# A streaming-encoder block on one core: a wider ramp in four stages, other rates for the adaLN tiles, and gate rows by way of DRAM

## The chip, the cores and the metric

The kernel runs on one core of one Trainium2 chip. The metric is the device time of one execution in microseconds, and the median of several executions stands for a kernel. The engines are TensorE (PE, with its weight loads shown as PEld), VectorE (DVE), ScalarE (ACT), GpSimd (POOL) and SyncE (SP). Lines such as L174 are lines of the kernel's source.

## The reference

One layer with three sublayers, over 256 tokens of 2048 channels in float32. Each sublayer normalises x, modulates it with a shift and a scale that come from the condition c by a large matrix (adaLN), and adds its result, multiplied by a gate that comes from c too.

```python
mod = (jax.nn.silu(c) @ w_ada[l] + b_ada[l]).reshape(B, N_SUBLAYERS, 3, D_MODEL)
shift, scale, gate = mod[:, :, 0], mod[:, :, 1], mod[:, :, 2]

def modulate(h, s):
    return _layer_norm(h) * (1.0 + scale[:, s, None, :]) + shift[:, s, None, :]

y = _swiglu(modulate(x, 0), ffn1_w13[l], ffn1_w2[l])
x = _layer_norm(ALPHA * x + FFN_WEIGHT * gate[:, 0, None, :] * y, ln_g[l, 0], ln_b[l, 0])

u = modulate(x, 1)
proj = u @ w_in[l] + b_in[l]
...
y = jnp.concatenate([h_m, h_r], axis=-1) @ w_out[l]
x = _layer_norm(ALPHA * x + gate[:, 1, None, :] * y, ln_g[l, 1], ln_b[l, 1])

y = _swiglu(modulate(x, 2), ffn2_w13[l], ffn2_w2[l])
x = _layer_norm(ALPHA * x + FFN_WEIGHT * gate[:, 2, None, :] * y, ln_g[l, 2], ln_b[l, 2])
```

`_swiglu` is `(silu(u @ w1) * (u @ w3)) @ w2` with 5632 inner columns. The mixer between the two FFNs makes q, k, v and gates of an mLSTM (four heads) and of a gated linear recurrence (RG-LRU) from one projection.

## The kernel before

**Weight tiles.** Every weight is read once, in tiles of 128 x 2048 float32 (1 MB). `load` (L81) takes one of four buffers named raw and issues the DMA on SP's queue; `split` (L88) makes a high part on ACT (L95) and the rest, a low part, on DVE (L97). High and low parts have three buffers each. A product is three matmuls: high by high, low by high, high by low (`mov_t`, L279, and L625 to L627 in the ramp). So a tile of the FFNs gives 24 matmuls of 128x128 by 128x512. Products collect in the eight PSUM banks.

**adaLN tiles.** The condition's matrix comes as 144 tiles of 1 MB, each with the 128 columns of one (sublayer, shift/scale/gate, channel tile) for all 2048 inputs. `ada_tile` (L170) loads one into a raw buffer, by the same queue, and DVE multiplies it by the broadcast silu(c) (`scb`, made at L148 to L155) and sums along the row (L174): one column of `adac`. Their order is fixed: for each sublayer the 32 of shift and scale, then the 16 of the gate. They are strewn among the weight tiles: `load` calls `tick` (L182), which adds the present rate to a credit and loads one adaLN tile for each whole credit. `ada_until` (L177) loads, at once, all that are still missing up to a given one. The rates are RAMP_RATE, FFN1_RATE, MIX_RATE and FFN2_RATE; FFN1's credit is set to zero after its last but one group, and the mixer and FFN2 begin at -2.

**Ramp.** FFN1 can't begin with a whole contraction, since that needs shift and scale of all 16 channel tiles. So the first 24 of its 44 tiles of inner columns (12 units of 512 columns, gate parts and value parts by turns, in 6 blocks) are done in five stages over 2, 3, 3, 4 and 4 channel tiles. After each stage a unit's partial sum is added to a home in SBUF: the two halves of `yacc`, `gate`, and x itself, which is reloaded later (`fetch`, L678). Units 0 and 1 stay in PSUM. `modulate` (L233) makes the modulated, transposed and split inputs for the next stage, two units before a stage ends, after an `ada_until` for that stage. In the last stage blocks 0 to 3 go through `gated` (silu on ACT, product on DVE) and, two tiles later, `turn` (transposes on PE, split on ACT and DVE). Blocks 4 and 5 do so in `g1(2)`.

**FFN after the ramp.** Groups of eight inner tiles: `g1` makes a group's inner activations, `g2` of the group before multiplies them by w2 and adds to `yacc`. At the last but one group `gate_rows` spreads the gate to all partitions, and `residual` (L322) adds gate times `yacc` to x. The last tiles are handled by `boundary` (L343), an order written out by hand: last products, residual, LayerNorm, modulation for the next sublayer and its first products.

**Gate rows.** `gate_rows` (L189) calls `rows_of` four times: each makes 512 columns of the broadcast gate row by four fp32 matmuls of a stretched column by the identity, and ACT copies the bank to `gate`. It is called three times; `rows_of` also makes `scb`.

**Mixer.** Output gates (w_vo), 25 projection tiles of one kind (`proj`, L796, with 16 x 2 matmuls each), gates and recurrence on DVE and ACT among them; then `ada_until` for the gate's columns and `gate_rows` (L931), v, k, q with the heads, and 16 tiles of w_out. Before the last four w_out tiles stands an `ada_until` for all of the third sublayer's shift and scale (L1041).

Each engine's instructions run in one order, which a planner with a model of times sets before the run; only the instructions of the boundaries and some others are pinned to the program's order.

Of the kernel before, what the change touches and what calls it, by code (L numbers as in the profile page):

```python
# [11 lines left out]
F32 = mybir.dt.float32  # L12
# [39 lines left out]
def block_kernel(ctx: ExitStack, tc: tile.TileContext, a: dict, out: bass.AP):  # L52
# [5 lines left out]
    sm = ctx.enter_context(tc.tile_pool(name="sm", bufs=4))  # L58
    ph = ctx.enter_context(tc.tile_pool(name="ph", bufs=1))

    def slot(name, dtype=F32):
# [79 lines left out]
    def rows_of(ps, col):  # L141

        for k in range(4):
            nc.tensor.matmul(ps[:, k * P:(k + 1) * P], col[:, k:k + 1].to_broadcast([P, P]), ident,
                             start=True, stop=True)

# [42 lines left out]
    def gate_rows(s, weight):  # L189

        for n in range(4):
            ps = bank(f"adag{s}{n}")
            rows_of(ps, adac[:, s, 2, 4 * n:4 * n + 4])
            nc.scalar.mul(gate[:, n * 512:(n + 1) * 512], ps, weight)

# [336 lines left out]
    def ffn(s, w13, w2, start, following=None):  # L532
# [23 lines left out]

        def gated(b, g, v):

            hth, htl = hts[4 * b // GRP]
            i = 4 * b % GRP  # L560
            sgs = []
            for t in range(NT):
                sg = sm.tile([P, 512], F32, tag="u", bufs=2, name=f"sg{s}{b}{t}")
                nc.scalar.activation(sg, g[t], AF.Silu)
                nc.vector.tensor_mul(sg, sg, v[t])
                sgs.append(sg)

            def turn():
                for t in range(NT):
                    tk = slice(t * P, (t + 1) * P)  # L570
                    ps = bank(f"th{b}{t}")
                    for j in range(4):
                        nc.tensor.transpose(ps[:, j * P:(j + 1) * P], sgs[t][:, j * P:(j + 1) * P], ident)
                    ps = ps.rearrange("p (a b) -> p a b", a=4)
                    nc.scalar.copy(hth[:, i:i + 4, tk], ps)
                    nc.vector.tensor_sub(htl[:, i:i + 4, tk], ps, hth[:, i:i + 4, tk].bitcast(F32))

            later(2, turn)

        units = RAMP // 2  # L580
        room = [r[:, 512 * i:512 * (i + 1)] for r in (*yacc, gate) for i in range(4)]
        room += [x[:, i // 4, 512 * (i % 4):512 * (i % 4 + 1)] for i in range(8)]
        part = [None, None] + [room[2 * i:2 * i + 2] for i in range(units - 2)]

        def ramp(ns):

            kept = {}
            n_w = k0 = 0
            ns, rest = ns()
            for st, k in enumerate(STAGES):  # L590
# [54 lines left out]
                for q in range(units):  # L645
# [11 lines left out]
                    if q not in kept:  # L657
                        for ps, p in zip(pss, part[q]):
                            if first:
                                nc.scalar.copy(p, ps)  # L660
                            else:
                                nc.vector.tensor_add(p, p, ps)
                    if last and q % 2 and q < 8:
                        gated(q // 2, *(kept.get(i) or part[i] for i in (q - 1, q)))
                k0 += k

        def g1(gi):
            grp = groups[gi]
            if start and gi == 2:
                new_h(gi)  # L670
                gated(4, part[8], part[9])
                later(4, lambda: (gated(5, part[10], part[11]), fetch()))
                return
            for b in range(grp[0] // 4, grp[-1] // 4 + 1):
                if b or start:
                    rows_block(b)

        def fetch():  # L678

            if True:  # L680
                with tc.issue_after(evac[-1].ins):
                    nc.scalar.dma_start(bq, a["b_s"])
                    nc.scalar.dma_start(rgp, a["rgp"])
                for t in range(NT):
                    nc.scalar.dma_start(x[:, t, :], a["x"][t * P:(t + 1) * P, :])
                scale_x()

# [40 lines left out]
        for gi in range(done, len(groups)):  # L728
# [438 lines left out]
```

## Time and profile before

| | |
|---|---|
| runs | 1980.02, 1989.11, 1979.78 us, median 1980.02 |
| profiled execution | 1983.66 us, of which span 1981.9 us |
| mean granted TensorE clock | 0.982 |
| DMA | 512.71 MB, mean 259 GB/s |
| adaLN reductions on DVE (L174) | 144, 338.9 us |

The span is cut into 40 slices of 49.5 us in the page's second part, where each digit is a busy share in tenths. In the lists of groups a row gives line, engine, operation, output and inputs with their shapes, how often, busy time and mean ns of one, and the idle time of the engine before them with what ended it. In the list of waits a row gives who waited for whom, the sum in us, how often, and the longest. Rows of the queues give the start and length of an issue; several in a row are merged, with their count.

### The profile page before, as it was taken

What the parts mean: (1) busy time and instruction counts of PE and PEld (TensorE: products, weight loads), DVE (VectorE), ACT (ScalarE), POOL (GpSimd) and SP (SyncE); (2) the same over time, 40 slices, a digit from 0 to 9 for tenths busy, and PEclk for the clock granted to TensorE, in tenths of its full rate; (3) what the DMA queues carried; (4) which work ended last, traced back from release to release, by engine and by line L of the source; (5) the groups of instructions that cost most, each with busy time, mean ns of one, the idle gap of its engine ahead of it and who ended that gap; (6) DMA issues with size and microseconds to landing.
All of it is one profiled execution on the core that took longest, in us unless ns stands there. A gap on an engine that the chain in (4) does not pass through costs nothing.

```text
span 1981.9 us, 21425 instructions
## 1 busy us (share of the span) xinstructions
PE 1895.1 (96%) x8680; PEld 1566.3 (79%) x8680; DVE 1422.6 (72%) x1360; ACT 846.1 (43%) x813; POOL 36.5 (2%) x59
## 2 busy tenths in 40 slices
PE   6999999999999999999899958999999999999997
PEld 5788888888878887788688846788888888888885
DVE  7899997867767668699987796556655644544656
ACT  5434444534333345655543317543444333334340
POOL 0000000000000000000000120000000000000000
PEclk8999999999999999999999989999999999999998
DMA  9999888878777564588886685566666655554552
GB/s 376 343 349 338 317 306 327 316 284 309 297 298 283 219 228 172 217 302 314 317 317 255 232 322 208 195 250 252 226 258 248 235 198 187 189 195 178 191 213 85
DMA packets 72675, 512.71 MB, mean 259 GB/s; under 512 B 8448, under 2 KB 8576, under 8 KB 10880
## 3 DMA queue, kind: packets, MB, share of 16 engines
q1 hardware_dynamic: 70848, 507.54, 68.5%
q10 hardware_dynamic: 1728, 3.80, 0.6%
q8 instruction: 68, 1.11, 0.2%
q14 instruction: 31, 0.25, 0.0%
HBM read 509.22 MB, written 2.10 MB: 258 GB/s over the span
## 4 chain that ended last, share of the span: by engine, by line
PE 67%; DVE 13%; DMA 11%; issue 6%; ACT 3%; POOL 0%; DVEq 0%; SPq 0%; ACTq 0%
DMA ada<-in_w_ada 10%; PE fv L287 5%; PE fv L288 5%; PE fv L286 5%; PE py L287 4%; PE py L286 4%; PE py L288 4%; PE fg L288 4%; PE fg L287 4%; PE fg L286 4%; PE rp L626 4%; PE rp L625 4%; PE rp L627 4%; DVE ada L174 3%; PE pj L276 3%
## 5 line engine op out<-in xcount | busy, mean ns | idle before, releaser
L174 DVE CUSTOM_DVE_ANT_0 ada<-ada,scb,badac 128x2048 f32<-128x2048 f32 x144 | 338.9, 2358 | 101.1 <-DMA ada<-in_w_ada 99.4
L97 DVE TENSOR_TENSOR lw<-rw,hw 128x2048 fp32r<-128x2048 f32 x80 | 183.1, 2291 | 123.3 <-ACT hw L95 123.3
L95 ACT CAST hw<-rw 128x2048 fp32r<-128x2048 f32 x80 | 153.1, 1913 | 239.7 <-PE py L288 116.1
L97 DVE TENSOR_TENSOR lfv<-rfv,hfv 128x2048 fp32r<-128x2048 f32 x64 | 146.2, 2291 | 132.8 <-ACT hfv L95 132.8
L95 ACT CAST hfg<-rfg 128x2048 fp32r<-128x2048 f32 (+1 forms) x64 | 117.0, 1833 | 203.4 <-PE fv L288 83.8
L287 PE MATMUL fv<-lfv,u 128*128 128x512 f32 x512 | 200.4, 391 | 3.3 <-DVE lfv L97 3.3
L95 ACT CAST hfv<-rfv 128x2048 fp32r<-128x2048 f32 x64 | 122.4, 1913 | 189.0 <-PE fg L288 145.0
L286 PE MATMUL fv<-hfv,u 128*128 128x512 f32 x512 | 199.3, 390 | 2.3 <-ACT hfv L95 2.3
L97 DVE TENSOR_TENSOR lfg<-rfg,hfg 128x2048 fp32r<-128x2048 f32 x60 | 137.2, 2290 | 88.3 <-ACT hfg L95 88.3
L288 PE MATMUL fv<-hfv,u 128*128 128x512 f32 x512 | 199.8, 390 | 0.0
L286 PE MATMUL py<-hw,hth 128*128 128x512 f32 x512 | 199.7, 391 | 0.0
L287 PE MATMUL py<-lw,hth 128*128 128x512 f32 x512 | 199.4, 389 | 0.1
L288 PE MATMUL py<-hw,htl 128*128 128x512 f32 x512 | 199.3, 389 | 0.0
L287 PE MATMUL fg<-lfg,u 128*128 128x512 f32 x496 | 193.7, 391 | 1.1 <-DVE lfg L97 1.1
L286 PE MATMUL fg<-hfg,u 128*128 128x512 f32 x496 | 194.6, 392 | 0.0
L288 PE MATMUL fg<-hfg,u 128*128 128x512 f32 x496 | 193.6, 390 | 0.0
L276 PE MATMUL pj<-u,hs 128*128 128x512 f32 x512 | 180.5, 398 | 0.0
L95 ACT CAST hra<-rra 128x2048 fp32r<-128x2048 f32 (+1 forms) x51 | 92.1, 1812 | 131.0 <-PE rp L627 71.3
L277 PE MATMUL pj<-u,ls 128*128 128x256 f32 x512 | 142.9, 280 | 0.0
L625 PE MATMUL rp<-hra,u 128*128 128x512 f32 x320 | 124.1, 396 | 6.9 <-ACT hra L95 5.2
L626 PE MATMUL rp<-lra,u 128*128 128x512 f32 x320 | 125.6, 394 | 0.7 <-DVE lra L97 0.7
L627 PE MATMUL rp<-hra,u 128*128 128x512 f32 x320 | 125.2, 393 | 0.0
(362 smaller groups left out, 3431.8 us busy)
## 6 DMA issues: line engine op xcount, KB each, us to landing
ada<-in_w_ada SPq DMA_DIRECT2D x144, 1024.0 KB, 5.4
rw<-in_w SPq DMA_DIRECT2D x80, 1024.0 KB, 4.8
rfg<-in_w SPq DMA_DIRECT2D x64, 1024.0 KB, 4.8
rfv<-in_w SPq DMA_DIRECT2D x64, 1024.0 KB, 4.8
rra<-in_w_r SPq DMA_DIRECT2D x48, 1024.0 KB, 6.4
rs<-in_w_s SPq DMA_DIRECT2D x32, 1024.0 KB, 4.9
rwo<-in_w_out SPq DMA_DIRECT2D x16, 1024.0 KB, 5.1
ro<-in_w_vo SPq DMA_DIRECT2D x8, 1024.0 KB, 4.8
```

Source lines behind the costliest of these rows:

```text
L95: act.copy(cut(hi, w), like(raw[:, w], hi))
L97: low.tensor_sub(cut(lo, w), like(raw[:, w], lo), cut(hi, w).bitcast(F32))
L174: nc.vector.tensor_tensor_reduce(raw, raw, scb, 1.0, badac[:, s, j, kt:kt + 1], ALU.mult, ALU.add, adac[:, s, j, kt:kt + 1])
L276: nc.tensor.matmul(ps, hi[:, w], u2[:, k].rearrange("p w b -> p (w b)"), start=k == 0, stop=False)
L277: nc.tensor.matmul(ps[:, 0:S], lo[:, w], uh[:, k, :], start=False, stop=k == KT - 1)
L286: nc.tensor.matmul(o, acth[:, k0 + j, tk], cut(hi, w), start=first and j == 0, stop=False)
L287: nc.tensor.matmul(o, acth[:, k0 + j, tk], cut(lo, w), start=False, stop=False)
L288: mm = nc.tensor.matmul(o, actl[:, k0 + j, tk], cut(hi, w), start=False, stop=last and j == 3)
L625: nc.tensor.matmul(pss[t], uh[:, k0 + j, tk], hi[:, w], start=a0 and j == j0, stop=False)
L626: nc.tensor.matmul(pss[t], uh[:, k0 + j, tk], lo[:, w], start=False, stop=False)
L627: mm = nc.tensor.matmul(pss[t], ul[:, k0 + j, tk], hi[:, w], start=False, stop=a1 and j == j0 + nj - 1)
```

## The change

Seven things change together.

- The ramp takes 32 inner tiles (16 units, 8 blocks) in four stages over 2, 4, 5 and 5 channel tiles. Blocks 6 and 7, which `g1(3)` used to make, move into it.
- The homes of the partial sums are two spare slots (blocks 1 and 2), `yacc[0]`, `gate`, `yacc[1]` and both halves of x (blocks 3 to 7). In the last stage blocks 4 to 7 are gated in place, and their `turn` comes in `g1(2)` and `g1(3)`. The second half of the inner activations' slots is taken in block 2's `turn`. x is reloaded at `g1(3)`.
- The rates of adaLN tiles per weight tile are others: the ramp's, 0.68 for 0.6 in FFN1 and 0.76 for 0.55 in the mixer.
- The credit is no longer set to zero after the FFNs' last but one group.
- `gate_rows` makes one transpose of the 16 gate columns, one small ACT multiplication, a DMA of the 16 x 128 result to a line in DRAM and a DMA that reads that line into all 128 partitions; both are issued by POOL.
- `rows_of`, now only for `scb`, uses transposes in place of matmuls.
- At the start the first adaLN tile and b_ada are issued ahead of x.

```diff
-STAGES = (2, 3, 3, 4, 4)
-RAMP = 24
+STAGES = (2, 4, 5, 5)
+RAMP = 32
...
-RAMP_RATE = (1.0, 0.67, 0.89, 0.67, 0.6)
-FFN1_RATE = 0.6
-MIX_RATE = 0.55
+RAMP_RATE = (1.0, 0.63, 0.6, 0.6)
+FFN1_RATE = 0.68
+MIX_RATE = 0.76
...
         for k in range(4):
-            nc.tensor.matmul(ps[:, k * P:(k + 1) * P], col[:, k:k + 1].to_broadcast([P, P]), ident,
-                             start=True, stop=True)
+            nc.tensor.transpose(ps[:, k * P:(k + 1) * P], col[:, k:k + 1].to_broadcast([P, P]), ident)
...
     def gate_rows(s, weight):
-        for n in range(4):
-            ps = bank(f"adag{s}{n}")
-            rows_of(ps, adac[:, s, 2, 4 * n:4 * n + 4])
-            nc.scalar.mul(gate[:, n * 512:(n + 1) * 512], ps, weight)
+        pt = bank(f"adag{s}")
+        nc.tensor.transpose(pt[0:KT, 0:P], adac[:, s, 2, :], ident)
+        row = sm.tile([KT, P], F32, tag="grow", bufs=1, name=f"grow{s}")
+        nc.scalar.mul(row, pt[0:KT, 0:P], weight)
+        line = dram.tile([1, D], F32, name=f"line{s}")
+        nc.gpsimd.dma_start(line.rearrange("o (k p) -> (o k) p", p=P), row)
+        nc.gpsimd.dma_start(gate, line.to_broadcast([P, D]))
...
         units = RAMP // 2
-        room = [r[:, 512 * i:512 * (i + 1)] for r in (*yacc, gate) for i in range(4)]
-        room += [x[:, i // 4, 512 * (i % 4):512 * (i % 4 + 1)] for i in range(8)]
-        part = [None, None] + [room[2 * i:2 * i + 2] for i in range(units - 2)]
+        blocks = RAMP // 4
+        room, sgs = {}, {}
+
+        def rooms():
+
+            extra = [slot(f"extra{i}")[:, 0:D] for i in range(2)]
+            homes = [None, extra[0], extra[1], yacc[0], gate, yacc[1], x[:, 0, :], x[:, 1, :]]
+            for b in range(1, blocks):
+                q4 = [homes[b][:, 512 * i:512 * (i + 1)] for i in range(4)]
+                room[2 * b], room[2 * b + 1] = q4[0:2], q4[2:4]
...
                 if last:
                     new_h(0)
-                    new_h(1)
...
-                    if last and q % 2 and q < 8:
-                        gated(q // 2, *(kept.get(i) or part[i] for i in (q - 1, q)))
+                    if last and q % 2:
+                        b = q // 2
+                        g, v = (kept.get(i) or room[i] for i in (q - 1, q))
+                        if b == 2:
+                            gated(b, g, v, fresh=1)
+                        elif b < 4:
+                            gated(b, g, v)
+                        else:
+                            sgs[b] = room[9] if b == 5 else g
+                            for t in range(NT):
+                                nc.scalar.activation(sgs[b][t], g[t], AF.Silu)
+                                nc.vector.tensor_mul(sgs[b][t], sgs[b][t], v[t])
...
-            if start and gi == 2:
+            if start and gi in (2, 3):
                 new_h(gi)
-                gated(4, part[8], part[9])
-                later(4, lambda: (gated(5, part[10], part[11]), fetch()))
+                b = 2 * gi
+                later(1, lambda: turn(b, sgs[b]))
+                later(3, lambda: turn(b + 1, sgs[b + 1]))
+                if gi == 3:
+                    later(3, fetch)
                 return
...
                 if gi == len(groups) - 2:
-                    credit[:] = 0.0, 0.0
                     for t in range(NT):
...
     def start():
+        nc.scalar.dma_start(badac.rearrange("p a b c -> p (a b c)"), a["b_ada"])
+        nc.vector.tensor_scalar_add(badac[:, :, 1, :], badac[:, :, 1, :], 1.0)
+        ada_tile()
         for t in range(NT):
             for c in range(0, D, 1024):
                 nc.sync.dma_start(x[:, t, c:c + 1024], a["x"][t * P:(t + 1) * P, c:c + 1024])
-        nc.scalar.dma_start(badac.rearrange("p a b c -> p (a b c)"), a["b_ada"])
-        nc.vector.tensor_scalar_add(badac[:, :, 1, :], badac[:, :, 1, :], 1.0)
```

`turn` was a function inside `gated` and is now one beside it, so that the ramp's later blocks can call it by themselves; what it does is the same.

More of the change, by code (lines that the diff above doesn't have):

```diff
@@ L555, in rows_block, with gated, turn @@
             gated(b, pg, pv)
-        def gated(b, g, v):
+        def gated(b, g, v, fresh=None):
+            sg = []
+            for t in range(NT):
+                w = sm.tile([P, 512], F32, tag="u", bufs=2, name=f"sg{s}{b}{t}")
+                nc.scalar.activation(w, g[t], AF.Silu)
+                nc.vector.tensor_mul(w, w, v[t])
+                sg.append(w)
+            later(2, lambda: turn(b, sg, fresh))
+        def turn(b, sg, fresh=None):
+            if fresh is not None:
+                new_h(fresh)
@@ L559, in gated @@
             hth, htl = hts[4 * b // GRP]
             i = 4 * b % GRP
-            sgs = []
             for t in range(NT):
[L563 to L576, printed above, removed]
@@ L578, in gated @@
-            later(2, turn)
-        units = RAMP // 2
-        room = [r[:, 512 * i:512 * (i + 1)] for r in (*yacc, gate) for i in range(4)]
-        room += [x[:, i // 4, 512 * (i % 4):512 * (i % 4 + 1)] for i in range(8)]
-        part = [None, None] + [room[2 * i:2 * i + 2] for i in range(units - 2)]
+                tk = slice(t * P, (t + 1) * P)
+                ps = bank(f"th{b}{t}")
+                for j in range(4):
+                    nc.tensor.transpose(ps[:, j * P:(j + 1) * P], sg[t][:, j * P:(j + 1) * P], ident)
@@ L657, in ramp @@
                     if q not in kept:
-                        for ps, p in zip(pss, part[q]):
+                        for ps, p in zip(pss, room[q]):
                             if first:
@@ L662, in ramp @@
                                 nc.vector.tensor_add(p, p, ps)
[L663 to L664 removed]
+                    if last and q % 2:
[7 more added lines that the diff above has]
+                            sgs[b] = room[9] if b == 5 else g
+                            for t in range(NT):
+                                nc.scalar.activation(sgs[b][t], g[t], AF.Silu)
+                                nc.vector.tensor_mul(sgs[b][t], sgs[b][t], v[t])
                 k0 += k
@@ L678, in fetch @@
         def fetch():
[L680 to L686, printed above, removed]
+            with tc.issue_after(evac[-1].ins):
+                nc.scalar.dma_start(bq, a["b_s"])
+                nc.scalar.dma_start(rgp, a["rgp"])
+            for t in range(NT):
+                nc.scalar.dma_start(x[:, t, :], a["x"][t * P:(t + 1) * P, :])
+            scale_x()
         def g2(gi):
```

5 lines of the change are left out of this document (added).

## The prediction

> **What bounds the kernel now.** I began with the page's first parts: how full each engine is, and where in the span TensorE is not.
>
> ```profile
> PE 1895.1 (96%) x8680; PEld 1566.3 (79%) x8680; DVE 1422.6 (72%) x1360; ACT 846.1 (43%) x813; POOL 36.5 (2%) x59
> PE   6999999999999999999899958999999999999997
> ```
>
> TensorE (PE) is full almost everywhere, so this is a PE-bound kernel with holes: 1981.9 - 1895.1 = 87 us without a matmul. No change here removes a weight tile's matmul, so what is to be won is holes, the half-speed spells behind them, and small PE work. I then asked for busy time by stretch (columns: stretch, its length, PE busy, weight loads, DVE, ACT, POOL, granted clock, DMA share, GB/s).
>
> ```profile
> 0.00:62.00 62.00, 41.86 (x169) 33.16 (x170) 47.61 (x47) 35.27 (x49) 2.31 (x11) 0.89 0.96 373
> 62.00:223.00 161.00, 160.32 (x709) 132.48 (x708) 152.66 (x135) 63.02 (x45) 0.00 (x0) 0.99 0.92 342
> 283.00:640.00 357.00, 354.28 (x1603) 293.07 (x1602) 264.36 (x216) 147.34 (x108) 0.00 (x0) 1.00 0.80 302
> 640.00:725.00 85.00, 85.00 (x381) 70.46 (x380) 52.96 (x42) 30.76 (x19) 0.00 (x0) 1.00 0.58 211
> 830.00:926.00 96.00, 96.00 (x549) 83.92 (x549) 87.10 (x111) 54.60 (x64) 0.00 (x0) 1.00 0.82 304
> 926.00:976.00 50.00, 42.99 (x212) 35.79 (x211) 50.00 (x45) 24.73 (x28) 0.11 (x1) 0.93 0.84 313
> 976.00:1140.00 164.00, 163.49 (x848) 137.92 (x847) 134.61 (x184) 62.42 (x57) 9.34 (x18) 1.00 0.73 275
> 1167.00:1188.00 21.00, 0.00 (x0) 0.00 (x0) 20.01 (x20) 0.45 (x1) 4.53 (x2) 0.61 0.97 377
> ```
>
> Holes: 20 us at the start with DMA at its fastest; 0.7 us in the ramp; 2.7 us in FFN1 behind it; 7.0 us at 926:976 with DVE full; and 21 us at 1167:1188, where PE does nothing at all while DVE and DMA are full. The list of waits names the last two, and the order of the SyncE queue (SPq) says why.
>
> ```profile
> PE tl L286 <- ACT hwo L95: 21.2, 1, 21.2
> PE pv L287 <- DVE lv L97: 4.8, 2, 3.8
> PE pv L286 <- ACT hv L95: 2.2, 1, 2.2
> ...
> ACT hwo L95 <- DVE adac L174: 34.9, 1, 34.9
> ...
> 910.55 23.02 SPq L173 DMA_DIRECT2D ada<-in_w_ada  x8
> ...
> 1144.75 33.42 SPq L173 DMA_DIRECT2D ada<-in_w_ada  x12
> 1180.70 7.15 SPq L85 DMA_DIRECT2D rwo<-in_w_out  x4
> ```
>
> Twelve adaLN tiles stand in one run ahead of the last four w_out tiles; PE wants those at 1167, they are issued at 1180.70. Eight more stand ahead of the v tiles. The code gives the same counts: a weight load adds the rate to a credit, each whole credit loads one adaLN tile, and ada_until forces what is missing. I counted calls in the loops. FFN1 ends with 80 tiles; 21 weight loads later, 21 x 0.55 - 2 = 9.55, so 89, where 96 are needed: 7 forced (the eighth came by credit). Another 36 loads make 116, where 128 are needed: 12 forced.
>
> **The change, part by part.** *Mixer's end.* With the new rates the ramp ends at 46 tiles, FFN1's other 64 loads add 43 (0.68 each): 89, nine more than needed. In the mixer 21 x 0.76 - 2 = 13.96: 102, so none is forced; 36 loads later 130, so none again. Both runs go. The hole at 1167 goes whole, and so does the cold start after it:
>
> ```profile
> 1188.22 1.22 PE L286 MATMUL tl<-hwo,rh 128*128 128x512 f32 x2 [21.23 <-ACT hwo L95]
> ...
> 1190.09 0.63 PE L286 MATMUL tl<-hwo,rh 128*128 128x512 f32 x1
> 1190.52 0.63 PE L287 MATMUL tl<-lwo,rh 128*128 128x512 f32 x1
> ...
> 1192.39 0.39 PE L286 MATMUL tl<-hwo,rh 128*128 128x512 f32 x1
> 1192.63 0.39 PE L287 MATMUL tl<-lwo,rh 128*128 128x512 f32 x1
> ```
>
> Starts are 0.43 us apart for the first nine, then 0.23: 9 x 0.2 = 1.8. Sum 21.2 + 1.8 = -23.0. Next in line there would be the four w_out tiles' splits on DVE; with twelve reductions gone (row below, 28 us of DVE) they run ahead of PE. The boundary chain after it stays.
>
> *Mixer's middle.* At 926:976, 7.0 us of hole, and some 2 us by the granted clock of 0.93 over the stretch. DVE is full there, and the v phase gets three more adaLN tiles than before, so I keep 2 us of it lost: -7, between 0 and -9.
>
> *Gate rows.* The old way is 16 fp32 matmuls, two instructions each, on an engine that is full at two of the three places and late at the third.
>
> ```profile
> L144 PE MATMUL adag<-ident,adac 128*128 128x128 f32 x96 | 11.5, 275 | 0.0
> L573 PE MATMUL th<-ident,sg 128*128 128x128 f32 x176 | 22.8, 272 | 0.0
> L174 DVE CUSTOM_DVE_ANT_0 ada<-ada,scb,badac 128x2048 f32<-128x2048 f32 x144 | 338.9, 2358 | 101.1 <-DMA ada<-in_w_ada 99.4 <-ACT scb L155 1.7
> ```
>
> A transpose costs 22.8/176 = 0.13; three of them replace 11.5: -11.1. The price is delay: two DMAs, each waited for on POOL's queue, which has 59 instructions in the whole span and none from 283 to 725 (x0 above), so nothing of weight is queued behind the wait. The nearest rows are a load of 8 KB and the 1 MB row broadcasts from the other queues.
>
> ```profile
> sc<-in_c ACTq DMA_DIRECT2D x1, 8.0 KB, 4.2
> ln_g<-in_ln_g SPq DMA_DIRECT2D x3, 1024.0 KB, 5.5
> L326 DVE TENSOR_TENSOR gy<-yacc,gate x16: 685/690/693, 634.3 to 1864.8; 128x512 f32<-128x512 f32 x16
> L194 ACT ACTIVATE gate<-adag x12: 590/597/600, 618.4 to 1813.3; 128x512 f32<-128x512 f32 x12
> ```
>
> In FFN1 the column is ready by 618.4; 0.6 + 4.2 + 5.5 makes about 629, and DVE first reads the gate at 634.3. Five us to spare: cost 0. Were the cover gone, the reader would block DVE and the splits queued behind it. [...]
>
> *Ramp.* PE is at 160.32 of 161 there, so a wider ramp can give 0.7 at most. DVE's adds into the partial sums go from 80 (four stages of 20) to 84 (three of 28) at about 0.69 (gy, of the same shape, above), spread over 56 weight tiles where there were 42: less load per us. I take 0.
>
> *Start.* The first hole is DMA's: at 373 GB/s a 1 MB tile takes 2.81 us. Before, the last weight tile of stage 0 is the 19th MB (2 of x, 11 adaLN, 6 weights); after, the 23rd (2, 13, 8). That is 11.2 us later, and PE has two more tiles, 2 x 24 x 0.227 = 10.9, to do meanwhile. The hole stays, and so does this wait, 4.0 us of it in one piece: +0.3.
>
> ```profile
> PE rp L625 <- ACT hra L95: 5.2, 2, 4.0
> ```
>
> x moves behind one adaLN tile (2.8 us later), but the first weight tile is the 6th MB in both, so that is hidden; the broadcast of c takes 16 instructions fewer on an idle PE. I take +1, between -3 and +5.
>
> *Pressure.* 0.68 for 0.6 and 0.76 for 0.55 put more tiles between weights. FFN1's row lost 2.7 of 357 us at 0.6, the ramp's 0.7 of 161 at 0.67 to 0.89; the former carried over 600 us is 4.5, of which 2.7 are paid now, and 640:725, which carried no adaLN tiles, has DVE to spare. I take +3; ends are 0 and the ring rival's +50 below. Moving the reload of x to a later group, the in-place partial sums, and the credit no longer reset cost nothing: x has over 20 weight tiles (110 us) before its first reader.
>
> Sum: -23.0 - 7 - 11.1 + 3 + 1 = -37.1. The profiled execution took 1983.66, so 1946.6; it stood 3.6 above the runs' median of 1980.02, so I predict 1943.
>
> **The rivals.** *The ring (slower).* Raw tiles share four buffers, so an adaLN tile that lands late holds up weights. Its issues in FFN1 and in the ramp:
>
> ```profile
> 446.41 0.33 SPq L173 DMA_DIRECT2D ada<-in_w_ada  x1
> 448.61 0.33 SPq L85 DMA_DIRECT2D rfv<-in_w  x1
> 453.80 0.33 SPq L173 DMA_DIRECT2D ada<-in_w_ada  x1
> 456.00 0.33 SPq L85 DMA_DIRECT2D rfv<-in_w  x1
> 461.19 0.33 SPq L85 DMA_DIRECT2D rw<-in_w  x1
> 463.39 0.33 SPq L173 DMA_DIRECT2D ada<-in_w_ada  x1
> ...
> 100.92 0.33 SPq L173 DMA_DIRECT2D ada<-in_w_ada  x1
> 103.79 0.33 SPq L85 DMA_DIRECT2D rra<-in_w_r  x1
> 107.19 0.33 SPq L173 DMA_DIRECT2D ada<-in_w_ada  x1
> ```
>
> With one weight between two adaLN tiles 7.39 us, with two 9.59. If that is the loop's own speed: at rate r an interval holds 1/r weights on average, so 1/r - 1 of the intervals hold two, and a weight costs r x (7.39 x (2 - 1/r) + 9.59 x (1/r - 1)) = 5.19 r + 2.2 us: 5.31 at 0.6 (below PE's 24 x 0.227 = 5.45), 5.73 at 0.68, 6.14 at 0.76 (a projection tile takes PE 96/549 x 32 = 5.6). It decides from r = 0.63 on: 64 x 0.28 + 53 x 0.54 = +47, less the pressure already counted, about 1987; with the mixer's middle hole kept, 1994. For it: FFN1 lost 2.7 already. Against it: in the ramp the same interval took 6.27 and PE was full. 0.05.
>
> *DVE gives it back.* The mixer's middle hole only moves, and the higher rate costs 7 more: 1943 + 7 + 7 = 1957 (1954 to 1966). For it: 50.00 of 50 on DVE. 0.15.
>
> *Late gate rows.* The broadcast waits its turn on POOL, and DVE stops at the first gy. Two of the three gates (the mixer's reader stands far behind, in w_out) come 10 us after their reader instead of 5 before; PE has split tiles in hand for a fourth of that: +15, 1958. For it: DVE is busy 264 of 357 us there. Against it: the 5 us to spare. [...] 0.05.
>
> *It does not do what it says.* The planner's order keeps a run of adaLN tiles ahead of the last w_out tiles although none is forced: only the gate rows are won, 1973. 0.05.
>
> *A better start.* The 4.0 us wait above and a cold spell behind it, some 2 to 4 us, close as well, and the middle goes whole: 11 to 18 less than the forecast, 1925 to 1932. For it: DMA is at 0.96, not 1, up to 62. Against it: the count of MB. 0.06.
>
> **How the numbers follow.** The forecast, 1932 to 1954, holds 0.64; the bounds of the middle, start and pressure make its width. The range 1928 to 1966 takes in the DVE and gate rivals and half of the better start; left out are the ring, the run that stays, and some edges, about 0.18. A measurement tells 0.5% from no change, 9.9 us: faster below 1970 is 0.64 + 0.15 + 0.05 + 0.06 = 0.90; same 0.05 (the run that stays); slower 0.05 (the ring).
>
> **What would show it.** Right: no run of more than two adaLN issues between 900 and 1200, no wait of PE's tl above 3 us, adag with 3 instructions and no DVE wait on gate. Wrong: a PE wait on lfg, lfv or lw that sums above 6 us in FFN1 (ring); DVE full and PE below 95% somewhere in 830 to 1140 (DVE); a gy that waits for a DMA (gate). The start is wrong if the first 80 us lose more than 5 us beyond today's.

## The result and the profile after

| | before | after |
|---|---|---|
| median of the runs | 1979.90 us (1978.72 to 1989.11) | 1953.96 us (1953.27 to 1956.92) |
| profiled execution, its span | 1983.66, 1981.9 | 1956.92, 1955.1 |

The ratio of the times is 0.9862, with a 95% interval of 0.9831 to 0.9893. The forecast was 1943, so it asked for 10.4 us more than came: 37.1 less by the profiled executions, against 26.7. The measured 1953.96 lies inside the stated 1928 to 1966, but at the upper end of the forecast's own 1932 to 1954, and nearer to the 1957 of the rival by which DVE gives the gain back than to 1943.

Of the page of the changed kernel, first TensorE's total and its 40 slices, then the small rows of the issues by POOL (what is moved, queue, count, KB each, us from issue to landing).

```profile
PE 1881.4 (96%) x8571; PEld 1554.9 (80%) x8571; DVE 1425.5 (73%) x1364; ACT 847.8 (43%) x814; POOL 43.3 (2%) x65
PE   5899999999999999899989898999999999999997
```

```profile
line<-grow POOLq DMA_DIRECT2D x3, 8.0 KB, 5.7
gate<-line POOLq DMA_DIRECT2D x3, 1024.0 KB, 7.4
```

Of the 87 us without a matmul, 1955.1 - 1881.4 = 74 are left. The dip at 1167 is gone, but the second slice and those around 806, 1000 and 1100, full before, now show 8. The stretches of the prediction again, for the changed kernel (the last one is the 21 us before its `tl` begins, where the hole was):

```profile
0.00:62.00 62.00, 39.95 (x161) 32.22 (x162) 41.66 (x41) 34.26 (x47) 4.28 (x11) 1.00 0.88 339
62.00:223.00 161.00, 155.31 (x682) 127.55 (x681) 139.99 (x116) 67.26 (x53) 0.00 (x0) 0.98 0.88 331
283.00:640.00 357.00, 357.00 (x1617) 296.33 (x1616) 293.65 (x253) 153.86 (x118) 1.30 (x2) 1.00 0.83 316
640.00:725.00 85.00, 85.00 (x380) 70.47 (x379) 75.40 (x63) 32.39 (x20) 0.00 (x0) 1.00 0.91 343
830.00:926.00 96.00, 96.00 (x547) 84.27 (x546) 90.31 (x111) 55.42 (x63) 0.00 (x0) 1.00 0.83 309
926.00:976.00 50.00, 50.00 (x241) 41.61 (x241) 49.95 (x47) 27.62 (x30) 1.25 (x3) 1.00 0.88 334
976.00:1140.00 164.00, 154.03 (x789) 130.00 (x788) 140.90 (x192) 61.19 (x55) 11.54 (x19) 0.97 0.78 292
1147.00:1168.00 21.00, 21.00 (x94) 17.39 (x93) 17.04 (x20) 10.04 (x14) 4.60 (x2) 1.00 0.69 255
```

The first two rows together lose 27.7 us without a matmul where before lost 20.8: PE begins later (below, under the start), and the wait of 4.0 us that stood at 58 us is now one of 5.4 at 75, and so in the second row. Then three things changed places. FFN1 is full: 357.00 of 357, at the higher rate. The holes at 926:976 and at the mixer's end are closed. But 976:1140, where PE had lost 0.5 us, now loses 10.0 (164 - 154.03), at a granted clock of 0.97. The list of waits says on whom (its first line belongs to the start):

```profile
PE tu L243 <- ACT n L1092: 10.9, 2, 8.5
...
PE pn L998 <- DVE misc L990: 5.0, 1, 5.0
PE pj L279 <- ACT rh L943: 5.0, 1, 5.0
...
PE po L290 <- DVE lo L98: 3.4, 1, 3.4
```

`pn` and `pj` did not wait so before; `po` waited 1.1 and this `tu` 2.1; no wait of `tl` on hwo stands in the list any more. To place them I cut both traces at the same products, and each segment lasts from one to the next (the last column is the best variant of the experiments). The names are those of the products' banks: `po` belongs to the output gates, `pj` to the projections, `pv` to v, `pn` to the heads, `pw` to w_out, `tl` to a boundary's last tiles, `fg` to an FFN's gate parts, and `tu` to transposes of the normalised x.

| segment, by PE's products | before | after | best variant |
|---|---|---|---|
| start to boundary 0's first `tl` (start, ramp, FFN1) | 708.0 | 706.0 | 699.4 |
| boundary 0, to the first `pj` | 132.8 | 137.6 | 133.4 |
| projections, to the first `pv` | 103.1 | 97.0 | 98.2 |
| v | 51.5 | 44.4 | 44.2 |
| k and q, to the first `pw` | 98.7 | 104.8 | 98.5 |
| heads and w_out, to the last `pw` | 72.9 | 80.0 | 74.9 |
| hole before boundary 1's `tl` | 21.2 | -0.2 | -0.2 |
| boundary 1, to the first `fg` of FFN2 | 31.5 | 26.5 | 26.3 |
| FFN2 | 681.5 | 678.2 | 678.3 |
| the rest | 80.7 | 80.8 | 80.8 |

So 44.9 us were won (2.0 + 6.1 + 7.1 + 21.4 + 5.0 + 3.3) and 18.1 given back in three places (4.8 + 6.1 + 7.1, and 0.1 at the end). The first of those three is on SP's queue, at boundary 0 (start, length, engine, instruction):

```profile
799.30 0.33 SPq L173 DMA_DIRECT2D ada<-in_w_ada  x1
806.68 0.33 SPq L86 DMA_DIRECT2D ro<-in_w_vo  x1
```

The mixer's credit starts at -2 and four loads add 0.76 each: 1.04, so one adaLN tile goes ahead of the last w_vo tile. On DVE a wait of 3.25 us for its DMA and its reduction stand in front of that boundary's split of `lo`, for which PE waits 3.4 us:

```profile
804.29 2.35 DVE L174 CUSTOM_DVE_ANT_0 ada<-ada,scb,badac 128x2048 f32<-128x2048 f32 x1 [3.25 <-DMA ada<-in_w_ada]
...
806.57 2.29 DVE L98 TENSOR_TENSOR lo<-ro,ho 128x2048 fp32r<-128x2048 f32 x1
...
808.91 0.79 PE L290 MATMUL po<-lo,u 128*128 128x512 f32 x1 [3.40 <-DVE lo L98]
```

The second place, in the changed kernel's timeline of DVE, ACT and PE:

```profile
1008.66 2.35 DVE L174 CUSTOM_DVE_ANT_0 ada<-ada,scb,badac 128x2048 f32<-128x2048 f32 x1
...
1010.93 0.69 DVE L942 SCALAR_TENSOR_TENSOR t<-t,xc 128x512 f32<-128x512 f32 x1
1011.54 2.48 DVE L967 TENSOR_TENSOR v<-pv,bv 128x512 f32<-128x512 f32 x4
1011.65 0.62 ACT L943 CAST rh<-t 128x512 fp32r<-128x512 f32 x1 [0.50 <-DVE t L942]
...
1012.37 0.77 PE L279 MATMUL pj<-u,hs 128*128 128x512 f32 x1 [4.97 <-ACT rh L943]
...
1015.07 0.63 PE L279 MATMUL pj<-u,hs 128*128 128x512 f32 x1
```

ACT's `rh` is named, but ACT waited for DVE's `t`, and `t` and the bias of v (L967) stood behind a reduction of 2.35 us. After the wait PE's products take 0.63 until 1015.7 in place of 0.40. At 1109.45 it is the same with `misc` behind a reduction at 1100.32 and a split at 1106.45. The gate's way in the same kernel, at the first gate:

```profile
617.90 0.27 PE L192 MATMUL adag<-ident,adac 128*16 128x128 f32 x1
...
619.92 0.26 ACT L194 ACTIVATE grow<-adag 16x128 f32<-16x128 f32 x1
620.48 0.73 POOL L196 DMA_DIRECT2D line<-grow  x1 [599.45 <-ACT grow L194]
...
626.87 0.57 POOL L197 DMA_DIRECT2D gate<-line  x1 [5.66 <-PE py L291]
```

And who reads the gate (the first number after the times is the first start), from the view by tile:

```profile
L329 DVE TENSOR_TENSOR gy<-yacc,gate x16: 682/684/693, 636.2 to 1837.9; 128x512 f32<-128x512 f32 x16
```

The 7.4 us of the page is a median of three. By the trace's landing times this first broadcast took 9.0 us and landed at 635.9, and `gy` starts at 636.2: in time, but with 0.3 us to spare where the forecast had 5. FFN2's landed at 1797.8, 0.1 us ahead of its reader at 1797.9; the mixer's has 185 us.

### The profile page after: what moved, and what is told of

It reads as the page before. It is cut to its first block, busy times and chain, and to the rows that moved or that the text cites. A ratio compares the mean times of both kernels' runs of the same rounds, so it can differ in the third digit from the quotient of the medians.

```text
span 1955.1 us, 21210 instructions
## 1 busy us (share of the span) xinstructions
PE 1881.4 (96%) x8571; PEld 1554.9 (80%) x8571; DVE 1425.5 (73%) x1364; ACT 847.8 (43%) x814; POOL 43.3 (2%) x65
## 4 chain that ended last, share of the span: by engine, by line
PE 78%; DVE 9%; DMA 6%; ACT 4%; issue 3%; POOL 0%; DVEq 0%; SPq 0%; ACTq 0%
PE py L290 6%; PE py L289 6%; PE py L291 6%; PE fv L290 5%; PE fv L291 5%; PE fv L289 5%; PE fg L291 5%; PE fg L290 5%; PE fg L289 5%; PE pj L279 5%; DMA ada<-in_w_ada 3%; PE rp L639 3%; PE rp L640 3%; PE rp L638 3%; PE pj L280 2%
## 5 line engine op out<-in xcount | busy, mean ns | idle before, releaser
L98 DVE TENSOR_TENSOR lfv<-rfv,hfv 128x2048 fp32r<-128x2048 f32 x56 | 128.2, 2291 | 126.0 <-ACT hfv L96 125.9
L96 ACT CAST hra<-rra 128x2048 fp32r<-128x2048 f32 (+1 forms) x67 | 122.8, 1837 | 173.0 <-PE rp L640 140.0
L98 DVE TENSOR_TENSOR lfg<-rfg,hfg 128x2048 fp32r<-128x2048 f32 x52 | 119.1, 2291 | 88.5 <-ACT hfg L96 88.5
L638 PE MATMUL rp<-hra,u 128*128 128x512 f32 x448 | 172.0, 395 | 5.6 <-ACT hra L96 5.4
L289 PE MATMUL fv<-hfv,u 128*128 128x512 f32 x448 | 174.7, 391 | 2.3 <-ACT hfv L96 2.3
L290 PE MATMUL fv<-lfv,u 128*128 128x512 f32 x448 | 175.2, 391 | 1.6 <-DVE lfv L98 1.6
L639 PE MATMUL rp<-lra,u 128*128 128x512 f32 x448 | 174.8, 391 | 0.3 <-DVE lra L98 0.3
L291 PE MATMUL fv<-hfv,u 128*128 128x512 f32 x448 | 174.9, 390 | 0.0
L640 PE MATMUL rp<-hra,u 128*128 128x512 f32 x448 | 174.2, 391 | 0.0
L289 PE MATMUL fg<-hfg,u 128*128 128x512 f32 x432 | 169.6, 392 | 0.0
L291 PE MATMUL fg<-hfg,u 128*128 128x512 f32 x432 | 168.9, 391 | 0.0
L290 PE MATMUL fg<-lfg,u 128*128 128x512 f32 x432 | 168.7, 391 | 0.0
L98 DVE TENSOR_TENSOR lra<-rra,hra 128x2048 fp32r<-128x2048 f32 (+1 forms) x67 | 146.7, 2192 | 20.7 <-ACT hra L96 20.7
```

What stands on the lines that cost most here:

```text
L96: act.copy(cut(hi, w), like(raw[:, w], hi))
L98: low.tensor_sub(cut(lo, w), like(raw[:, w], lo), cut(hi, w).bitcast(F32))
L289: nc.tensor.matmul(o, acth[:, k0 + j, tk], cut(hi, w), start=first and j == 0, stop=False)
L290: nc.tensor.matmul(o, acth[:, k0 + j, tk], cut(lo, w), start=False, stop=False)
L291: mm = nc.tensor.matmul(o, actl[:, k0 + j, tk], cut(hi, w), start=False, stop=last and j == 3)
L638: nc.tensor.matmul(pss[t], uh[:, k0 + j, tk], hi[:, w], start=a0 and j == j0, stop=False)
```

## The experiments

Medians below are of runs on one chip beside runs of the kernel before, and the ratios are to that kernel. The batches' medians of before were 1981.01 (the first four variants), 1983.87 (the next four) and 1981.92 (the last three). The changed kernel was in none of these batches, and its own ratio is known to 6 us either way, so a difference from it by medians tells little below that: the ratios give 0.4, 4.4, 10.5 and 9.9 us where the medians below give 0.8, 4.8, 9.7 (the old gate rows) and 8.4 (the short reductions). Smaller effects rest on the segments of the traces.

**x first again.**

```diff
     def start():
-        nc.scalar.dma_start(badac.rearrange("p a b c -> p (a b c)"), a["b_ada"])
-        nc.vector.tensor_scalar_add(badac[:, :, 1, :], badac[:, :, 1, :], 1.0)
-        ada_tile()
         for t in range(NT):
...
+        nc.scalar.dma_start(badac.rearrange("p a b c -> p (a b c)"), a["b_ada"])
+        nc.vector.tensor_scalar_add(badac[:, :, 1, :], badac[:, :, 1, :], 1.0)
```

> The changed kernel with one part undone: the start issues x first again, and the first adaLN tile after it. In the changed kernel's trace the first product of the ramp starts at 26.6 us (20.2 before), after an x that lands at 8.2 (4.8 before), statistics of x's second half that stand among two adaLN reductions on DVE, and a small POOL operation of 2.2 us. My theory: the adaLN tile ahead of x costs these 6 us, of which some 4 to 5 still stand at the end of the ramp. It expects the first product at 19 to 21 and about 1949.5 (1948 to 1951). The rival, that the wider first stage sets the start whatever comes first (the 23rd MB, as in the prediction), expects the first product earlier but the end of stage 0 and the time where they were, 1953 to 1955.

1953.20 us (1950.56 to 1956.54), 0.9860 [0.9842, 0.9878]: 0.8 less than after, not 4. In the trace the first product of the ramp is back at 20.1 from 26.6, the start of FFN2 is 3.2 us earlier (1192.9 for 1196.1), which the rival did not expect, and then the gain is lost within 44 us. These are the same stretch after FFN2's start, first in the changed kernel, then in this one:

```profile
1195.00:1239.00 44.00, 36.98 (x138) 25.41 (x138) 20.06 (x34) 31.72 (x63) 1.82 (x4) 0.92 0.33 120
```

```profile
1192.00:1236.00 44.00, 37.14 (x127) 24.98 (x128) 18.17 (x32) 29.73 (x62) 1.64 (x4) 0.84 0.34 120
```

PE is busy as long, but at 0.84 of full clock for 0.92 and with 11 matmuls fewer: 0.08 x 44 = 3.5 us. That looks like luck of the clock and not like a cost of this start; two later variants bear on it, the changed start at these rates and the best variant again.

**The mixer's credit.**

```diff
-                credit[:] = -2.0, MIX_RATE
+                credit[:] = -2.2, MIX_RATE
```

> The changed kernel with the mixer's credit beginning at -2.2 in place of -2.0. At -2.0 four loads of 0.76 make 1.04, so an adaLN tile is issued at 799.3 ahead of the last of the four output-gate tiles, while the boundary is still running; DVE then waits 3.25 us for it with a low part queued behind, and PE waits 3.4 us for that low part and runs 5 us at half speed. At -2.2 they make 0.84, and the tile comes one load later. My theory expects that wait of PE (po on lo) to fall to the 1.1 us of before, and 1949 to 1950. The rival, that DVE is late there for another reason (the order of the boundary or the two row loads), expects the wait to stay and 1953 to 1955.

1949.18 us (1947.07 to 1951.91), 0.9840 [0.9823, 0.9856]: 4.8 less than after. The waits of this variant:

```profile
PE pj L279 <- DVE v L967: 5.1, 1, 5.1
...
PE pn L998 <- DVE misc L990: 1.2, 1, 1.2
...
PE po L290 <- DVE lo L98: 1.1, 1, 1.1
```

Boundary 0 takes 132.8 us again. The wait in the heads went too, since the reductions now fall between other instructions there; the one in k stays.

**The mixer's old rate.**

```diff
-MIX_RATE = 0.76
+MIX_RATE = 0.55
```

> The changed kernel with the mixer's rate back at 0.55. By the count of loads 89 adaLN tiles are there when the mixer begins, 98 at its gate rows (none forced) and 118 at its end, so 10 are forced in one run ahead of the last w_out tiles. My theory has two parts. The run costs a hole there of 16 to 20 us with 2 us of half speed behind it; and the two waits that are new in the changed kernel (PE 5.0 us for a k projection's bank at 1007, 5.0 us for the heads' weights at 1104) come from the higher rate's reductions on a full DVE, so both fall below 1.5 us, which with their half-speed spells gives back 12. Sum: 1953.96 + 20 - 12 - 4 (no tile in the boundary: 4 x 0.55 - 2 is below 1) = 1958, 1953 to 1963. A rival, that the two new waits come from the planner's other order and not from the rate, expects them to stay: 1969 to 1973. A second rival, that the run at the end is hidden now, expects no hole: 1938 to 1943.

1960.84 us (1957.95 to 1964.66), 0.9893 [0.9874, 0.9912]. The run of adaLN tiles is back on SP's queue, ten long, and with it the hole; the list of waits of this variant begins so:

```profile
PE tl L289 <- ACT hwo L96: 15.0, 1, 15.0
```

The waits in k and the heads are gone, and k and q take 99.0 us and w_out 72.3. So the higher rate of the change takes 13.5 us there (5.8 + 7.7) and gives 21.3: the hole and 6.3 in the boundary behind it.

**The old gate rows.**

```diff
-        nc.tensor.transpose(pt[0:KT, 0:P], adac[:, s, 2, :], ident)
...
-        nc.gpsimd.dma_start(gate, line.to_broadcast([P, D]))
+        for n in range(4):
+            ps = bank(f"adag{s}{n}")
+            for k in range(4):
+                nc.tensor.matmul(ps[:, k * P:(k + 1) * P], adac[:, s, 2, 4 * n + k:4 * n + k + 1].to_broadcast([P, P]),
+                                 ident, start=True, stop=True)
+            nc.scalar.mul(gate[:, n * 512:(n + 1) * 512], ps, weight)
```

> The changed kernel with the old gate rows: 16 fp32 matmuls of a stretched column by the identity and four ACT multiplications, three times, and no DMA of POOL. My theory: the new rows are worth the PE time of the old ones, 11.5 us less 0.4, all of it on a full PE, so 1965 (1963 to 1967). A rival, that the old rows fell into holes in the mixer, expects two thirds of it, 1961.5. Another, that the new rows' DMAs cost something somewhere (the gate's line takes 5.7 us to land, POOL waits), expects less than 7, below 1961.

1963.64 us (1963.17 to 1966.57), 0.9915 [0.9899, 0.9931]: 9.7 more than after. FFN1 ends 3.6 us later, the projections, where the mixer's gate rows stand, take 3.7 more and FFN2 3.2. By the profiled executions it is only 6.2 in all, since k, q, boundary 0 and the heads took 3.9 less in this one.

**The rates alone.** The kernel before with two numbers changed.

```diff
-FFN1_RATE = 0.6
-MIX_RATE = 0.55
+FFN1_RATE = 0.68
+MIX_RATE = 0.76
```

> The kernel before with the two adaLN rates of the change alone (FFN1 0.68, mixer 0.76): old ramp, old gate rows, old start. 3 adaLN tiles are left for the mixer's end where before forced 8 and the changed kernel forces none. My theory (rates carry the gain, the ramp is worth nothing, the start order costs 3 that FFN2 hides, gate rows carry 9.7): 1954 + 9.7 - 3 (x first) + up to 5 for the 3 forced tiles = 1960 to 1966, and the first half of the segment from the last tw product to tl1 keeps a hole of 0 to 6 us. Rival, the ramp itself carries a gain of some us (more tiles, fewer slots waited for): 1966 to 1974. Rival, the rates do not pay without the other parts: 1974 to 1981.

1968.87 us (1966.26 to 1973.35), 0.9932 [0.9910, 0.9954]: above what I expected, in the range of the rival that credits the ramp. Its profile stands 3.6 us above that of the old gate rows, which differs from it by the ramp, the start and the credit that is kept. The two are within 0.8 us of each other from boundary 0's first `tl` to the last `pw`, 2.0 apart at FFN2's start, where this one's three forced tiles stood on SP's queue shortly before, and FFN2 adds 1.6. In FFN1 this one lost 3.7 of the 357 us of 283:640, waiting for `lfg` and `lfv`, where the other, with the new ramp, lost none; its earlier start makes up for it. The whole is too little to tell by, and the ramp got a run of its own below.

**The ring, and the mixer at a lower rate.** 97 adaLN tiles are in at FFN1's end where the changed kernel has 89, so eight move out of the mixer (the expectation's 13 was a miscount). x comes first, as above.

```diff
-FFN1_RATE = 0.68
-MIX_RATE = 0.76
+FFN1_RATE = 0.8
+MIX_RATE = 0.61
...
-                credit[:] = -2.0, MIX_RATE
+                credit[:] = -2.2, MIX_RATE
```

> The changed kernel with x loaded first again, the mixer's credit at its start -2.2 for -2, FFN1's rate 0.8 for 0.68 and the mixer's 0.61 for 0.76: the same number of adaLN tiles in all, some 13 of them moved from the mixer's k, q and heads parts into FFN1, none forced at the mixer's end. My theory (DVE's reductions in front of rh, t and misc make the two 5 us waits in k and heads; FFN1 has room, PE being full there): both waits fall under 1.5 us, FFN1 stays full, median 1937 to 1944. Rival, the ring of four raw buffers of the prediction (5.19 x rate + 2.2 us for a weight, 6.35 us at 0.8 against 6.1 us of PE for it): PE waits on lfg, lfv or lw in FFN1 by 25 us or more in all, median 1965 to 2010. Rival, the waits in k and heads have another cause and stay: 1944 to 1950.

1939.03 us (1936.01 to 1940.51), 0.9777 [0.9759, 0.9795]. The stretches of this variant:

```profile
283.00:640.00 357.00, 357.00 (x1617) 296.32 (x1616) 304.62 (x265) 153.94 (x118) 1.30 (x2) 1.00 0.88 330
...
976.00:1070.00 94.00, 94.00 (x529) 80.85 (x528) 77.79 (x87) 38.83 (x36) 1.60 (x5) 1.00 0.83 311
```

FFN1 is full at 0.8, where the ring rival asked for 25 us or more (58 with the 5.45 us of PE for a tile that the prediction used), and k and q are full as well.

**Short reductions.** What is left out: from adaLN tile 89 on only 128 of 2048 columns are multiplied and summed, so part of the second sublayer's gate and all of the third's gate, shift and scale lack the rest.

```diff
+        w = 128 if i >= 89 else 2048
-        nc.vector.tensor_tensor_reduce(raw, raw, scb, ...)
+        nc.vector.tensor_tensor_reduce(raw[:, 0:w], raw[:, 0:w], scb[:, 0:w], ...)
```

> The changed kernel, in which adaLN tiles from index 89 on are reduced over 128 of their 2048 columns only (gate, shift and scale of the last sublayers are not the reference's); every load and its order is as in the changed kernel. If DVE's 2.35 us per tile in front of rh, v and misc makes the waits in k and heads and the half speed behind them, both waits (5.0 and 5.0 us) fall under 1.5 us, boundary 0's wait stays only as far as it is for the load, and the median is 1938 to 1946. If the loads (their place on SP's queue, their share of the DMA engines) make them, the waits stay and the median is 1950 to 1955.

1945.56 us (1940.70 to 1950.45), 0.9812 [0.9788, 0.9836]: 8.4 less than after, 6.5 by the profiled executions. What differs is DVE's time for a tile and, with it, when raw buffers come free. The stretch where after lost 10 us:

```profile
976.00:1140.00 164.00, 164.00 (x849) 138.29 (x848) 101.16 (x182) 60.59 (x51) 9.83 (x19) 1.00 0.81 310
```

The loads and their order are the same, DMA is at 0.81 for 0.78, and PE is full. Both waits left the list, and `po` waits 1.4. Boundary 0 stayed as long as after's, though (137.5 us): this profile loses the time before the first `o`, waiting on DVE 1.6 us for `lw` and 3.2 for `n`. So this run bears on k, q and the heads, and the one of the credit on boundary 0.

**The changed start at these rates.** As the last but one, without x first.

```diff
-FFN1_RATE = 0.68
-MIX_RATE = 0.76
+FFN1_RATE = 0.8
+MIX_RATE = 0.61
...
-                credit[:] = -2.0, MIX_RATE
+                credit[:] = -2.2, MIX_RATE
```

> As the last but one (credit -2.2, FFN1 0.8, mixer 0.61), but with the changed kernel's start (b_ada and an adaLN tile ahead of x). The first 3 us that x first gains were lost again to half clock at FFN2's start in the run that had x first alone. If that was the phase of the clock at that place and not the start, this kernel is 2 to 4 us slower than with x first (1940 to 1948). If what the start gains never reaches the end, because something later takes the time (a load that arrives at its own pace), both are within 1 us.

1944.11 us (1942.42 to 1947.53), 0.9810 [0.9790, 0.9831]: 5.1 above the variant with x first by the medians, 2.9 by the profiled executions. At the first `tl` the start's loss is 3.7 us. It does reach the end here, which fits that in the first variant FFN2's clock hid it.

**The old ramp.** The kernel before with `gate_rows` as in the change, 0.72 in FFN1, 0.61 and -2.2 in the mixer, and the credit kept after FFN1's last but one group.

```diff
 STAGES = (2, 3, 3, 4, 4)
 RAMP = 24
...
-FFN1_RATE = 0.6
-MIX_RATE = 0.55
+FFN1_RATE = 0.72
+MIX_RATE = 0.61
```

> Everything that the best version so far has (gate rows by way of DRAM, x first, mixer 0.61 with credit -2.2, no adaLN tile forced from FFN1's end on), but the old ramp of 24 tiles in five stages; FFN1's rate is 0.72, so that 98 adaLN tiles are in at its end against 97. If the ramp is worth nothing, as the prediction has it: within 2 us of the repeat of the best version run beside it. Rival, the wider ramp gains by ending later, when FFN1's first groups no longer wait for lfg and lfv (5.5 us of such waits in the run of the rates alone, 1.6 with the new ramp): 3 to 6 us slower, with the waits there to be seen, and the last product of FFN1 later by as much.

1938.66 us (1935.38 to 1942.10), 0.9782 [0.9761, 0.9804], against 1937.17 for the repeat beside it: the ramp is worth 1.5 us by the medians, less than the spread, and nothing by the profiled spans (1933.6 for 1933.8). PE waits 2.0 us for `lfv` in all, 1.6 in the repeat, and FFN1 is full here too, so the rival falls beside these other parts. In the run of the rates alone the old ramp came with 3.7 us of such waits; what ended them here is not shown.

**More in FFN1 still.**

```diff
-FFN1_RATE = 0.8
-MIX_RATE = 0.61
+FFN1_RATE = 0.9
+MIX_RATE = 0.55
```

> The best version so far with FFN1's rate 0.9 for 0.8 and the mixer's 0.55 for 0.61: 103 adaLN tiles at FFN1's end for 97, none forced. The ring of the prediction would take 5.19 x 0.9 + 2.2 = 6.87 us for a weight against 5.45 of PE: some +90 us over 64 loads, with PE waiting on lfg, lfv and lw. My theory (DMA and DVE have room in FFN1 until the reductions fill DVE: 0.9 x 2.36 us is 0.24 us more for each weight tile of 5.45, on an engine at 264 of 357 us before): PE full in FFN1, and the mixer within 2 us of the repeat run beside it, since no wait on DVE over 1.5 us is left there at 0.61.

1945.96 us (1942.02 to 1949.99), 0.9825 [0.9805, 0.9846]. Both theories missed. The second half of FFN1 in this variant, then in the repeat at 0.8:

```profile
400.00:640.00 240.00, 238.78 (x1075) 196.97 (x1074) 202.82 (x175) 98.71 (x71) 1.30 (x2) 1.00 0.93 357
640.00:705.00 65.00, 63.36 (x276) 50.98 (x274) 59.90 (x50) 22.26 (x13) 0.00 (x0) 1.00 0.94 345
```

```profile
400.00:640.00 240.00, 240.00 (x1085) 199.14 (x1084) 198.28 (x169) 100.80 (x72) 1.30 (x2) 1.00 0.92 346
640.00:700.00 60.00, 60.00 (x266) 49.70 (x265) 54.49 (x47) 22.17 (x13) 0.00 (x0) 1.00 0.93 356
```

FFN1 ends 5.2 us later (first `tl` at 704.6 for 699.4), and boundary 0 adds 3.7. That is a limit between 0.8 and 0.9, but not the ring's price of 91 us. PE's waits there are for `lw` and `lfv` on DVE, 3.1 us in all, but behind them stand late loads: from 400 us on ACT's splits of weights waited 103.8 us for their DMA, 38.1 in the repeat. Whether it is the DMA engines, at 0.92 to 0.94 in both, or the four raw buffers that makes the loads late was not tried.

**The best variant again.** x first, -2.2, 0.8 and 0.61, as above.

> The best version so far again (x first, credit -2.2, FFN1 0.8, mixer 0.61), on the same chip as the two beside it: 1936 to 1942, ratio to before 0.976 to 0.980.

1937.17 us (1935.56 to 1939.33), 0.9775 [0.9757, 0.9794]: the lowest median of all, some 17 us below the changed kernel's. Its profile is the last column of the table of segments. The kernel is that of the ring's variant to the letter, yet FFN2 took 680.8 us in that one's profile and 678.1 in this one: 89.5 and 86.8 us up to its 300th product, and the same from there on. PE was busy 65.5 us of 1165:1240 in both, at a granted clock of 0.91 in that one and 0.95 in this. So 2.7 us come and go at FFN2's start with no change at all, about what hid the gain of x first.

## Why the prediction was right, and what it mis-sized

That the time fell inside the forecast's range is partly luck. One term came out 12 us too small and another 3, and some 5 us of gain that the sum did not have made up for part of it.

**Mixer's end, -23.0: right.** The hole of 21.2 us went whole, with the cold start behind it (a granted clock of 0.50 in 1188:1192 before): the hole and boundary 1 together lost 26.4. Of that, 3.4 are more than the forecast had, the rest of boundary 1 being shorter; why is not shown, only that it lengthens again with the run of tiles (32.8 for 26.5). The old mixer's rate brings the hole back. The rival by which the run of tiles stays has fallen with it.

**Mixer's middle, -7, and the gate rows, -11.1: right, a little low.** Projections and v gave 13.2 where the forecast has 7 and one of the three gates, 3.7. `adag` is down to three matmuls, and the old gate rows cost 9.7 by the medians. No `gy` of the changed kernel waited for a DMA, so the rival of the late gate rows has fallen, but narrowly: the first gate's two transfers took 5.8 and 9.0 us, not the 4.2 and 5.5 of the rows from the other queues, and the 5 us to spare were 0.3, and 0.1 in FFN2. In the run with the old ramp a `gy` did wait 0.36 us. That the delay cost nothing was close to luck. From the first issue to the second landing the trace shows 15.4, 13.6 and 9.2 us for the three gates. Whether DVE's work or busier DMA engines (a share of 0.86 and 0.95 in 620:636 and 937:952, 0.76 in 1788:1799) made the first two longer is not shown.

**Ramp, 0: right.** The run with the old ramp is 1.5 us from its twin, which has 97 adaLN tiles at FFN1's end for 98.

**Start, +1: too low.** The prediction counted MB for the weight tiles and took the later x for hidden. The chain through x's statistics was not: x lands at 8.2 for 4.8, and the statistics of its second half then share DVE with the first reductions. The changed kernel's timeline:

```profile
8.17 1.29 DVE L210 BATCH_NORM_STATS2 stx<-x 128x6 f32<-128x512 f32 x2 [8.17 <-DMA x<-in_x]
...
11.16 0.23 POOL L202 TENSOR_SCALAR vex<-mvx 128x1 f32<-128x1 f32 x1 [9.86 <-DVE mvx L215]
...
18.02 2.28 DVE L174 CUSTOM_DVE_ANT_0 ada<-ada,scb,badac 128x2048 f32<-128x2048 f32 x1
...
18.19 2.19 POOL L202 TENSOR_SCALAR vex<-mvx 128x1 f32<-128x1 f32 x1 [6.15 <-DVE mvx L215]
...
22.05 0.47 PE L243 MATMUL tu<-ident,n 128*128 128x128 f32 x1 [8.52 <-ACT n L1092]
```

The ramp's first product is 6.4 us later (26.65 for 20.22) and the 240th still 4.9 (94.1 for 89.2). The prediction had called the start wrong if the first 80 us lose more than 5 us beyond today's. By time without a matmul they do: 27.7 us for 20.1. By products the loss is just under 5, since the granted clock was 0.96 there for 0.89. At the 600th it is 3.6, and the pair of runs at 0.8 puts 2.9 to 5.1 on it.

**Pressure, +3: the step that failed.** It took the loss for one of FFN1, carried over from 2.7 us at 0.6. FFN1's loss went away (357.00 of 357; with the old ramp and these rates it was 3.7), and where the sum had +3, 18.0 us came up elsewhere: 4.8 at boundary 0, 6.1 in k and q, 7.1 in the heads and w_out. The mean of DVE there, 134.61 of 164 before, seemed to leave room; but three reductions of 2.35 us each stood just where an instruction of DVE releases PE, the one at boundary 0 with 3.25 us of waiting for its load besides. Each wait then costs more than itself: of the 6.1 us in k 5.0 are the wait, and the rest falls in the half speed behind it (a granted clock of 0.50 from 1012.37 to 1015.70). The runs divide it: the credit gives back 4.8, the short reductions clear k, q and the heads, the lower mixer rate does so with nothing left out.

**The other rivals.** The ring fell twice: no loss at 0.68, none at 0.8. So the intervals of 7.39 and 9.59 us, on which its price rested, were not the loop's own speed. "DVE gives it back" was right in kind, and by its number nearer than the forecast: it named the higher rate's cost on DVE at 7 us, where 18.0 came, but put the lost 7 us of the middle on top. The table could be read as its moving hole, 13.2 us won up to v's end and 13.2 lost behind. The run with the mixer's old rate parts the two: projections and v stay as short there (97.5 and 43.8 us) while the waits in k and the heads are gone. Its sign, PE below 95% with DVE full, came in part: PE at 94% in 976:1140, with DVE at 86% in the mean, and full in 1000:1015 (15.00 of 15) where PE has 10.03.

The sum by these terms, as measured: -2.0 up to boundary 0 (the start some +4, gate rows -3.6, FFN1's former stalls -2.7), +4.8, -13.2, +13.2, -26.4, -3.3 and +0.1, together -26.8, against 1981.9 - 1955.1.

## What to carry to other kernels

When filler work is spread among a kernel's loads by a rate, count not only the engine's mean load but what short instruction, on which PE waits, stands behind a piece of filler: one reduction of 2.35 us in the wrong place cost 5 to 7 us here (at boundary 0 with the wait for its load). Move the filler to the stage where PE has split tiles in hand (FFN1, full up to a rate of 0.8) rather than to where DVE sits in the chain (k, heads, boundaries). A run of forced work just before a boundary shows up on the DMA issue queue as one row with a large count, and was worth its whole hole here. A page's time to landing is a median: whether a transfer is in time is read from its own landing and its reader's start.

## What was not expected of the hardware

A POOL instruction of 0.23 us took 2.19 when it began beside a reduction on DVE, and ended with it (18.19 + 2.19 = 20.38, the reduction 18.02 + 2.28 = 20.30). An instruction of the same line at 1073.78 took 2.25 and ended at 1076.03, where the reduction beside it (1073.60 + 2.34) ended at 1075.94. What ties the two is not shown.

The half speed after a wait differs in length and can cancel a gain elsewhere: after 3.4 us of waiting at boundary 0 the products start 0.43 us apart, for 0.23 behind, from 808.91 to 814.19; after 5.0 us in k they run at half speed only from 1012.37 to 1015.70. The granted clock is 0.50 in both spells. So the shorter wait had the longer spell behind it, 5.3 us for 3.3; what sets the length is not shown. The 3.2 us that were gained by x first and lost to clock at FFN2's start, and the 2.7 us between two executions of the same kernel there, show that a change of a few us can disappear so.
